# Down projection of a SwiGLU block staged through five buffers instead of two, on one Trainium2 core

## The chip, the cores and the metric

The kernel runs on one core of one Trainium2 chip. The metric is the time of one execution in device microseconds; the number compared is the median of several runs. A profile of one further execution gives the rows shown below. TensorE (PE in the profile) multiplies, VectorE (DVE), ScalarE (ACT) and GpSimd (POOL) do the rest, and SyncE (SP), ScalarE and GpSimd issue DMAs.

## The reference

One layer of a decoder trunk, everything in float32, 512 tokens of width 2048:

```
h = rmsnorm(x);  x = x + concat(diff_attention(h), gated_retention(h)) @ w_o
x = x + cross_attention(rmsnorm(x), rmsnorm(mem))           # 256 memory tokens, 4 heads
hf = rmsnorm(x)
x = x + (silu(hf @ w_gate) * (hf @ w_up)) @ w_down          # D_FF = 5632
out = rmsnorm(x) * norm_f_g
```

The change concerns the last two lines and the hand-over to them.

## The kernel before

**Precision.** Each float32 operand is split into a high part, rounded to fp32r, and the rest: `split(hi, lo, src)` is a cast on ScalarE (L181) and a subtraction on VectorE (L182). A product is three matmuls (`mm3`, L190 to L192).

**Order.** The program order of each engine is what the code emits; no scheduler reorders it. The code builds a list of steps, `plan`, each of which uses one chunk of weights (512 KB). `run_plan` goes through it: first it emits loads (SP, L251) and the splits of weights up to two steps ahead (`split_more`), then the matmuls of the step (`use`), then for the last chunk of a group the evacuation of its PSUM banks (`evac`), and then it advances the generators in `side` by one yield each (`step_side`). A load goes into one of three raw buffers of 4 KB per partition, which comes free once the chunk in it has been split. Split weights of the feed-forward part have three places, so a split waits for the matmuls of the chunk three places before it.

**Feed-forward part.** D_FF is cut into eleven blocks of 512 columns (NB = 11). The order of blocks is gate 0, up 0, then for each b: gate b, down b-1, up b, and at the end gate 10, up 10, down 9, and down 10 fused with the final norm (`finish`).

- Gate and up are done with seven products per pair of k tiles (`seven_products`, matmuls of 256 columns at L888, eight chunks of 42 matmuls each). Their weights are combined and split in `combine_weights` (L266 to L272). The seven sums lie in seven PSUM banks until `fin` adds them on ScalarE and VectorE (L909 and L941, L899, L902). `plan_up` puts them in scratch: two stretches of `rest` at 12 and 14 KB (tag `u`) and the tile `live["u"]`. A generator (`rest_of`) then multiplies by the activated gate, splits the product into `a_h` and `a_l`, and sets `live["a_done"]`.
- Down of block b has four groups of 512 output columns, two chunks each, and four token tiles t with a bank each. The matmuls are 512 columns wide (`a_h`, `a_l` in the profile's names), 48 to a group. In the second chunk the token tiles come one after the other, so that their sums end one after the other. `fin` evacuates one: a scaled copy on ScalarE into a staging buffer (L974), and then an accumulating DMA from it, 256 KB into `y_d` in HBM, issued on GpSimd (L975).
- The staging buffer is `tmp()`: two buffers of 2 KB per partition at 28 and 30 KB of `rest`, taken in turn.
- All of gate, up and down take PSUM banks from one ring of eight (`any_bank`). Up after down takes first the four banks of down's third group and then three of its fourth.

**The end.** The last five steps (chunks of down 9) have eight chunks of down 10 interleaved in the list of loads and splits (`plan_last`). `finish` then loads `y_d` back, 1 MB per token tile (L999), multiplies down 10 (192 matmuls), adds (L1018), squares, normalises and stores (L1030). Its tiles for `y_d` take the memory that `live["u"]`, `a_h`, `a_l` and the third place had.

**The hand-over.** `turn_x` is a generator that transposes x to token order into `y_d`: four groups c of four transposes for each token tile t (L867), a copy (L870) and a DMA on GpSimd (L871). The fourth group has one bank (`spare`, bank 7), as gate 0 holds the others, and runs beside the first chunks of gate 0.

Of the kernel before, what the change touches and what calls it, by code (L numbers as in the profile page):

```python
# [20 lines left out]
P = 128  # L21
D = 2048
KT = D // P
T = 512
# [5 lines left out]
NB = DFF // 512  # L30
# [9 lines left out]
KB = 1024  # L40
# [38 lines left out]
def hybrid_block_kernel(ctx, tc, specs, x_t, mem_t, gains, norm_f_g, weights, alibi, decay, out):  # L79
# [9 lines left out]
    rest = const.tile([P, F_SIZE // 4], F32, name="rest")  # L89
# [1 line left out]
    xpool = top.enter_context(tc.tile_pool(name="xpool", bufs=1))  # L91

    bank = [psum.tile([P, 512], F32, name=f"bank{i}") for i in range(8)]
    turn = {"acc": 0, "aux": 0, "any": 0, "tmp": 0, "st": 0, "xst": 0, "yss": 0}

    def take(tag, n):
        turn[tag] += 1
        return (turn[tag] - 1) % n
# [10 lines left out]
    def shaped(flat, shape):  # L109
        if len(shape) == 2:  # L110
            return flat
        names = "abcd"[:len(shape) - 1]
        return flat.rearrange("p (" + " ".join(names) + ") -> p " + " ".join(names),
                              **dict(zip(names[1:], shape[2:])))

    def part(arena, at, shape):
        n = int(np.prod(shape[1:]))
        return shaped(arena[:, at // 4:at // 4 + n], shape)
# [56 lines left out]
    def tmp():  # L175
        return part(rest, F_TMP + take("tmp", 2) * 2 * KB, [P, T])
# [124 lines left out]
    def step_side():  # L301
        for g in list(side):
            if next(g, "end") == "end":
                side.remove(g)
# [47 lines left out]
    def cols(name, *pieces, row0=0):  # L352
        return lambda k0, nk: chunk(name, row0 + k0 * P, nk, pieces)
# [25 lines left out]
    def token_major(w, width, nk_total, lhs_of, ntok, finish, hook=None, bank=acc, ffn=False):  # L379

        nk = 1024 // width
        banks = {}
        for k0 in range(0, nk_total, nk):
            last = k0 + nk >= nk_total

            def use(hi, lo, k0=k0, last=last):
                for a, b in order(nk, ntok, last):
                    kk, t = (b, a) if last else (a, b)
                    if k0 == 0 and kk == 0:
                        banks[t] = bank(name="tm")  # L390
                    c = kk * width
                    mm3(banks[t][:, :width], lhs_of(k0 + kk, t), (hi[:, c:c + width], lo[:, c:c + width]),
                        k0 + kk == 0, k0 + kk == nk_total - 1)
            add(w(k0, nk), use,
                (lambda: [finish(t, banks[t]) for t in range(ntok)]) if last else None, hook if last else None, ffn=ffn)
# [129 lines left out]
    live = {}  # L525
# [330 lines left out]
    def spare(name=""):  # L856
        return bank[7]

    def turn_x():

        for c in range(4):
            while prep["ready"] < 4 * c + 4:
                yield
            for t in range(NT):
                ps = (acc if c % 2 == 0 else aux)() if c < 3 else spare()
                for k in range(4):
                    nc.tensor.transpose(ps[:, k * P:(k + 1) * P], xT[4 * c + k][:, t * P:(t + 1) * P], ident)  # L867
                yield
                st = tmp()
                nc.scalar.copy(st, ps)  # L870
                nc.gpsimd.dma_start(out=y_d[t * P:(t + 1) * P, c * 512:(c + 1) * 512], in_=st)  # L871
        live["turned"] = True
# [91 lines left out]
    def plan_down(b):  # L964
        for c0 in range(0, D, 512):
            def lhs(k, t):
                while live["a_done"] < b:
                    step_side()
                a = live["late"]
                return a[0][:, k, t * P:(t + 1) * P], a[1][:, k, t * P:(t + 1) * P]  # L970

            def fin(t, ps, c0=c0):
                st = tmp()
                nc.scalar.activation(st, ps, AF.Copy, scale=rx[:, t:t + 1])  # L974
                nc.gpsimd.dma_start(out=y_d[t * P:(t + 1) * P, c0:c0 + 512], in_=st, accum_op=ALU.add)  # L975
            token_major(cols("w_down", (c0, 512), row0=b * 512), 512, 4, lhs, NT, fin, bank=any_bank, ffn=True)
# [56 lines left out]
    def before(f):  # L1033
        marks.append((len(plan), f))
# [23 lines left out]
    def begin_pairs():  # L1058
        live.update(turned=False, late=None, g_done=-1, a_done=-1)
        start_prepare(prepare_pairs, G_FFN)  # L1060
        side.append(turn_x())
# [6 lines left out]
    def begin_late():  # L1068
        while not live["turned"] or prep["gen"] in side:
            step_side()  # L1070
        top.close()
        late = top.enter_context(tc.tile_pool(name="late", bufs=1))
        live["u"] = late.tile([P, 2, 256], F32, name="u3")
        live["late"] = [late.tile([P, 4, T], F32R, name=n) for n in ("a_h", "a_l")]
        third = late.tile([P, 14 * KB // 4], F32R, name="third")
        places["seven"].insert(0, (0, 14 * KB, third))

    before(begin_ffn)
    plan_gate(0)
    before(lambda: turn.update(any=8))  # L1080
    plan_up(0)
    marks.append((len(plan) - 5, begin_late))
    for b in range(1, NB):
        plan_gate(b)
# [58 lines left out]
```

## Time and profile before

| | |
|---|---|
| median of 3 runs | 2820.25 us (2817.19 to 2822.77) |
| the profiled execution | 2818.68 us, of which the span is 2816.3 us |
| mean granted TensorE clock | 0.985 |
| TensorE busy | 2707.0 us (96%) |
| VectorE busy | 1679.0 us (60%) |
| ScalarE busy | 1122.0 us (40%) |
| GpSimd busy | 150.4 us (5%) |
| evacuations of down (L974) | 160, 689 ns each |
| accumulating DMAs into `y_d` (L975, with 16 plain ones of L871) | 176, 256 KB, 5.4 us from issue to landing (median) |
| weight loads (L251) | 519, 512 KB, 3.4 us |

Busy times overlap, so they don't add up to the span. A matmul's end is modelled, so that a row of matmuls is best read from start to start. The rows that the prediction quotes are from the page, from lists of waits (who waited for whom: total us, times, longest us), from instructions in order of time (start, duration, and in brackets the idle time before and what ended it), and from stretches of time cut out of the trace.

### The profile page before, as it was taken

The numbers are of one execution on the slowest core, as the hardware profiler recorded it, in microseconds if no ns is written. First come the engines' busy times: TensorE is split into PE (matmuls) and PEld (weight loads), VectorE is DVE, ScalarE is ACT, GpSimd is POOL, SyncE is SP. The second block draws the span as 40 slices with busy tenths as digits, with TensorE's granted clock in tenths as the row PEclk, the third lists the DMA queues.
The fourth block names the chain that finished last, engine by engine and source line by source line (L and its number), as shares of the span: only waits on it lengthen the run. The fifth ranks groups of instructions, "written<-read, shape, count | busy, mean of one in ns | idle before, by whom it ended". The sixth has DMA issues, their size and how long they took to land.

```text
span 2816.3 us, 41803 instructions
## 1 busy us (share of the span) xinstructions
PE 2707.0 (96%) x17078; PEld 2449.3 (87%) x17078; DVE 1679.0 (60%) x2494; ACT 1122.0 (40%) x1550; POOL 150.4 (5%) x186
## 2 busy tenths in 40 slices
PE   9999999999999999999998999998989989999997
PEld 8999988888888888887898989898888979798985
DVE  6676444544554445746984756657475848484855
ACT  6555423333332223534534443443443434434433
POOL 0000000000000000000001010110101010101011
PEclk9999999999999999999999999999999999999998
DMA  7877642222222222233236364554546363637255
GB/s 243 291 243 235 219 164 83 89 88 89 95 90 95 88 96 89 90 100 117 98 111 144 110 146 120 128 127 126 132 113 152 109 142 120 143 106 150 98 151 170
DMA packets 124128, 373.16 MB, mean 132 GB/s; under 512 B 13472, under 2 KB 23712, under 8 KB 123424
## 3 DMA queue, kind: packets, MB, share of 16 engines
q1 hardware_dynamic: 96848, 314.88, 33.7%
q0 software_dynamic: 24640, 47.20, 11.4%
q10 hardware_dynamic: 2448, 8.43, 0.7%
q8 instruction: 133, 2.18, 0.3%
q14 instruction: 59, 0.48, 0.1%
HBM read 303.34 MB, written 67.11 MB: 132 GB/s over the span
## 4 chain that ended last, share of the span: by engine, by line
PE 46%; issue 41%; DVE 5%; POOL 5%; ACT 2%; DMA 1%; POOLq 0%; ACTq 0%; DVEq 0%
PE bank L190 15%; PE bank L192 15%; PE bank L191 15%; POOL y_d L975 5%; PE bank L888 1%; ACT ops L270 1%; DMA y_d<-rest 1%; DVE ops L272 1%; DVE rest L266 0%; DVE y L1018 0%; DVE rest L899 0%; DVE ops L182 0%; DMA rest<-in_norm_f_g_dram 0%; DVE rest L268 0%; DVE rest L269 0%
## 5 line engine op out<-in xcount | busy, mean ns | idle before, releaser
L190 PE MATMUL bank<-ops 128*128 128x512 f32 (+1 forms) x2504 | 858.4, 343 | 12.6 <-ACT ops L181 7.2
L191 PE MATMUL bank<-ops 128*128 128x512 f32 (+1 forms) x2504 | 851.3, 340 | 0.8 <-DVE ops L182 0.8
L192 PE MATMUL bank<-ops 128*128 128x512 f32 (+1 forms) x2504 | 851.7, 340 | 0.0
L182 DVE TENSOR_TENSOR ops<-rest,ops 128x1024 fp32r<-128x1024 f32 (+1 forms) x380 | 449.8, 1188 | 630.8 <-ACT ops L181 617.3
L888 PE MATMUL bank<-ops 128*128 128x256 f32 x5208 | 650.6, 285 | 66.1 <-ACT rest L974 56.4
L888 PEld LDWEIGHTS bank<-ops 128*128 128x128 f32 x5208 | 635.6, 193 | 76.6 <-ACT rest L974 60.8
L181 ACT CAST ops<-rest 128x1024 fp32r<-128x1024 f32 (+1 forms) x380 | 386.0, 1022 | 686.1 <-PE bank L191 354.1
L190 PEld LDWEIGHTS bank<-ops 128*128 128x128 f32 x2504 | 473.4, 189 | 69.1 <-ACT ops L181 8.1
L192 PEld LDWEIGHTS bank<-ops 128*128 128x128 f32 x2504 | 472.7, 189 | 53.8 <-DVE ops L182 0.2
L191 PEld LDWEIGHTS bank<-ops 128*128 128x128 f32 x2504 | 473.2, 189 | 52.8 <-DVE ops L182 1.4
L888 PE MATMUL bank<-ops,third 128*128 128x256 f32 x2184 | 265.5, 280 | 2.7 <-ACT rest L941 1.6
L888 PEld LDWEIGHTS bank<-ops,third 128*128 128x128 f32 x2184 | 260.4, 189 | 3.1 <-ACT rest L941 1.8
L974 ACT ACTIVATE rest<-bank,small 128x512 f32<-128x512 f32 x160 | 109.4, 689 | 288.9 <-DMA y_d<-rest 268.4
L270 ACT CAST ops<-rest 128x1024 fp32r<-128x1024 f32 x124 | 130.3, 1051 | 224.2 <-DVE rest L269 182.7
L975 POOL DMA_DIRECT2D y_d<-rest x160 | 138.7, 881 | 1271.3 <-ACT rest L974 1151.0
L271 DVE TENSOR_TENSOR ops<-rest,ops 128x768 fp32r<-128x768 f32 x124 | 118.2, 953 | 102.6 <-ACT ops L267 88.4
L272 DVE TENSOR_TENSOR ops<-rest,ops 128x1024 fp32r<-128x1024 f32 x124 | 152.0, 1226 | 31.0 <-ACT ops L270 29.2
L190 PE MATMUL bank<-ops,a_h 128*128 128x512 f32 x408 | 160.2, 393 | 4.0 <-ACT ops L181 4.0
L191 PE MATMUL bank<-ops,a_h 128*128 128x512 f32 x408 | 160.1, 393 | 0.5 <-DVE ops L182 0.5
L192 PE MATMUL bank<-ops,a_l 128*128 128x512 f32 x408 | 159.7, 391 | 0.0
L267 ACT CAST ops<-rest 128x768 fp32r<-128x768 f32 x124 | 103.4, 834 | 88.5 <-issue 51.8
L266 DVE TENSOR_TENSOR rest<-rest 128x512 f32<-128x512 f32 x176 | 121.4, 690 | 4.2
(138 smaller groups left out, 2062.9 us busy)
## 6 DMA issues: line engine op xcount, KB each, us to landing
rest<-in_weights_dram SPq DMA_DIRECT2D x519, 512.0 KB, 3.4
y_d<-rest POOLq DMA_DIRECT2D x176, 256.0 KB, 5.4
h_d<-rest ACTq DMA_DIRECT2D x16, 512.0 KB, 5.5
g_d<-rest SPq DMA_DIRECT2D x32, 256.0 KB, 5.1
rest<-g_d SPq DMA_DIRECT2D x16, 512.0 KB, 3.2
rest<-h_d SPq DMA_DIRECT2D x16, 512.0 KB, 3.3
xT<-in_x_t_dram SPq DMA_DIRECT2D x16, 256.0 KB, 5.8
y<-y_d SPq DMA_DIRECT2D x4, 1024.0 KB, 7.5
```

The lines of the kernel that those rows point to most:

```text
L181: nc.scalar.copy(hi, src)
L182: nc.vector.tensor_tensor(out=lo, in0=src, in1=hi.bitcast(F32), op=ALU.subtract)
L190: nc.tensor.matmul(out_ap, lh, rh, start=first, stop=False)
L191: nc.tensor.matmul(out_ap, lh, rl, start=False, stop=False)
L192: nc.tensor.matmul(out_ap, ll, rh, start=False, stop=last)
L266: nc.vector.tensor_tensor(out=w[:, 0:2], in0=q[:, 1:3], in1=q[:, 0:1].to_broadcast([P, 2, 256]), op=ALU.add)
L270: nc.scalar.copy(hi[:, 3:7], w)
L271: nc.vector.tensor_tensor(out=lo[:, 0:3], in0=q[:, 1:4], in1=hi[:, 0:3].bitcast(F32), op=ALU.subtract)
L272: nc.vector.tensor_tensor(out=lo[:, 3:7], in0=w, in1=hi[:, 3:7].bitcast(F32), op=ALU.subtract)
L888: nc.tensor.matmul(to, x[:, b, c], y[:, a], start=j == 0 and o == 0 and m == 0, stop=j == nj - 1 and m == 2, skip_group_check=True)
L974: nc.scalar.activation(st, ps, AF.Copy, scale=rx[:, t:t + 1])
L975: nc.gpsimd.dma_start(out=y_d[t * P:(t + 1) * P, c0:c0 + 512], in_=st, accum_op=ALU.add)
```

## The change

Down's evacuation takes its staging buffer from a ring of five: the two of `tmp()`, the two stretches of `rest` that up uses for its sums, and `live["u"]`. Before it does so it makes sure that up's generator has read its sums; only for the last down (block 9, which follows up 10) is there something left to emit. The transposes of the fourth group of `turn_x` begin one step later.

```
-    turn = {"acc": 0, "aux": 0, "any": 0, "tmp": 0, "st": 0, "xst": 0, "yss": 0}
+    turn = {"acc": 0, "aux": 0, "any": 0, "stage": 0, "tmp": 0, "st": 0, "xst": 0, "yss": 0}
...
 def turn_x():
         for c in range(4):
             while prep["ready"] < 4 * c + 4:
                 yield
+            if c == 3:
+                yield
             for t in range(NT):
...
 def plan_down(b):
             def fin(t, ps, c0=c0):
-                st = tmp()
+                while live["a_done"] < (b if b < NB - 2 else NB - 1):
+                    step_side()
+                st = live["stages"][take("stage", 5)]
                 nc.scalar.activation(st, ps, AF.Copy, scale=rx[:, t:t + 1])
                 nc.gpsimd.dma_start(out=y_d[t * P:(t + 1) * P, c0:c0 + 512], in_=st, accum_op=ALU.add)
...
 def begin_late():
         places["seven"].insert(0, (0, 14 * KB, third))
+        live["stages"] = [part(rest, at * KB, [P, T]) for at in (28, 30, 12, 14)]
+        live["stages"].append(live["u"].rearrange("p a b -> p (a b)"))
```

In the changed file the evacuation stands at L978, its DMA at L979, the load of `y_d` at L1003, the transposes at L869, and the matmuls of gate and up at L890.

ScalarE, first and second group of the first down, with what each instruction waits for. `DMASW0` to `DMASW7` are the semaphores that GpSimd's DMAs signal in turn, `DMAHW` those of the loads; `u_10492` is `live["u"]`. Before:

```order
L974 ACTIVATE rest<-bank_76,small 128x512 [waits PE_49]
L974 ACTIVATE rest<-bank_77,small 128x512 [waits PE_49]
L974 ACTIVATE rest<-bank_70,small 128x512 [waits DMASW0_49,PE_49,Activation_49]
L974 ACTIVATE rest<-bank_71,small 128x512 [waits DMASW1_49,PE_49,Activation_49]
L924 ACTIVATE rest<-rest 128x1024 [waits DVE_49]
L181 CAST third<-rest 128x1024 [waits DMAHW6_49]
L181 CAST ops<-rest 128x1024 [waits DMAHW7_49,PE_49]
L974 ACTIVATE rest<-bank_72,small 128x512 [waits DMASW2_49,PE_49,Activation_49]
L974 ACTIVATE rest<-bank_73,small 128x512 [waits DMASW3_49,PE_49,Activation_49]
```

After:

```order
L978 ACTIVATE rest<-bank_76,small 128x512 [waits PE_49]
L978 ACTIVATE rest<-bank_77,small 128x512 [waits PE_49]
L978 ACTIVATE rest<-bank_70,small 128x512 [waits PE_49]
L978 ACTIVATE rest<-bank_71,small 128x512 [waits PE_49]
L926 ACTIVATE rest<-rest 128x1024 [waits DVE_49]
L181 CAST third<-rest 128x1024 [waits DMAHW6_49,Activation_49]
L181 CAST ops<-rest 128x1024 [waits DMAHW7_49,PE_49,Activation_49]
L978 ACTIVATE u_10492<-bank_72,small 128x512 [waits PE_49]
L978 ACTIVATE rest<-bank_73,small 128x512 [waits DMASW0_49,PE_49,Activation_49]
```

The order is the same; before, the third evacuation waited for the DMA of the first; now the sixth does.

ScalarE at the first group of the last down (block 9), where the two casts `128x2x256` at a time are the halves of up 10's split. Before:

```order
L181 CAST ops<-rest 128x2x256 [waits DVE_49] x2
L181 CAST ops<-rest 128x1024 [waits DMAHW5_49,PE_49,Activation_49]
L974 ACTIVATE rest<-bank_73,small 128x512 [waits DMASW6_49,PE_49]
L974 ACTIVATE rest<-bank_74,small 128x512 [waits DMASW7_49,PE_49]
L974 ACTIVATE rest<-bank_75,small 128x512 [waits DMASW0_49,PE_49,Activation_49]
L974 ACTIVATE rest<-bank_76,small 128x512 [waits DMASW1_49,PE_49,Activation_49]
L181 CAST ops<-rest 128x2x256 [waits DVE_49] x2
```

After:

```order
L181 CAST ops<-rest 128x2x256 [waits DVE_49] x2
L181 CAST ops<-rest 128x1024 [waits DMAHW5_49,PE_49,Activation_49]
L181 CAST ops<-rest 128x2x256 [waits DVE_49] x2
L978 ACTIVATE u_10492<-bank_73,small 128x512 [waits DMASW3_49,PE_49]
L978 ACTIVATE rest<-bank_74,small 128x512 [waits DMASW4_49,PE_49]
L978 ACTIVATE rest<-bank_75,small 128x512 [waits DMASW5_49,PE_49]
L978 ACTIVATE rest<-bank_76,small 128x512 [waits PE_49]
```

The second pair of casts moved ahead of the four evacuations.

SP's queue at the end: the last load of weights, the four loads of `y_d` and the first store. Before:

```order
L251 DMA rest<-in_weights_dram 128x1024 [waits DMAHW6_49,DVE_49]
L999 DMA y_21595<-y_d 128x2048 [waits DMASW4_49,DMASW0_49,PE_49]
L999 DMA y_21596<-y_d 128x2048 [waits DMASW5_49,DMASW1_49]
L999 DMA y_21597<-y_d 128x2048 [waits DMASW6_49,DMASW2_49]
L999 DMA y_21598<-y_d 128x2048 [waits DMASW7_49,DMASW3_49]
L1030 DMA out_dram<-rest 128x512 [waits DVE_49]
```

After:

```order
L251 DMA rest<-in_weights_dram 128x1024 [waits DMAHW6_49,DVE_49]
L1003 DMA y_21595<-y_d 128x2048 [waits DMASW4_49,DMASW3_49,DMASW5_49,DMASW2_49,DMASW6_49,DMASW1_49,DMASW7_49,DMASW0_49,Activation_49]
L1003 DMA y_21596<-y_d 128x2048 [waits DMASW5_49,DMASW1_49]
L1003 DMA y_21597<-y_d 128x2048 [waits DMASW6_49]
L1003 DMA y_21598<-y_d 128x2048 [waits DMASW3_49]
L1034 DMA out_dram<-rest 128x512 [waits DVE_49]
```

The first load takes memory that is now the fifth stage, and waits for the last accumulating DMAs of all token tiles; the three others stand behind it.

More of the change, by code (lines that the diff above doesn't have):

```diff
@@ L93, in hybrid_block_kernel @@
     bank = [psum.tile([P, 512], F32, name=f"bank{i}") for i in range(8)]
-    turn = {"acc": 0, "aux": 0, "any": 0, "tmp": 0, "st": 0, "xst": 0, "yss": 0}
+    turn = {"acc": 0, "aux": 0, "any": 0, "stage": 0, "tmp": 0, "st": 0, "xst": 0, "yss": 0}
     def take(tag, n):
@@ L863, in turn_x @@
                 yield
+            if c == 3:
+                yield
             for t in range(NT):
@@ L972, in fin @@
             def fin(t, ps, c0=c0):
-                st = tmp()
+                while live["a_done"] < (b if b < NB - 2 else NB - 1):
+                    step_side()
+                st = live["stages"][take("stage", 5)]
                 nc.scalar.activation(st, ps, AF.Copy, scale=rx[:, t:t + 1])
@@ L1076, in begin_late @@
         places["seven"].insert(0, (0, 14 * KB, third))
+        live["stages"] = [part(rest, at * KB, [P, T]) for at in (28, 30, 12, 14)]
+        live["stages"].append(live["u"].rearrange("p a b -> p (a b)"))
     before(begin_ffn)
```

## The prediction

> **What bounds the kernel now.** I read the page first (shares, groups), then the waits, then the order of time on TensorE and ScalarE around one down projection, then stretches and DMA queues there.
>
> ```profile
> span 2816.3 us, 41803 instructions
> ...
> PE 2707.0 (96%) x17078; PEld 2449.3 (87%) x17078; DVE 1679.0 (60%) x2494; ACT 1122.0 (40%) x1550; POOL 150.4 (5%) x186
> ...
> L974 ACT ACTIVATE rest<-bank,small 128x512 f32<-128x512 f32 x160 | 109.4, 689 | 288.9 <-DMA y_d<-rest 268.4
> ```
>
> TensorE is the bound, but "busy" hides slow matmuls. The odd row is L974: 160 evacuations of down, before which ScalarE sits idle for 268.4 us because a staging buffer is still being read by its DMA. ScalarE is 40% busy, so that alone costs nothing; the question is who stands behind it. From TensorE's waits between 1400 and 2760 us (total, times, longest):
>
> ```profile
> PE bank L888 <- ACT rest L974: 56.4, 21, 5.4
> ```
>
> The products of gate and up (L888) wait 56.4 us for banks that down's evacuations hold. One such place, on TensorE:
>
> ```profile
> 1600.79 0.40 PE L190 MATMUL bank<-ops,a_h 128*128 128x512 f32 x1
> ...
> 1644.37 3.12 PE L888 MATMUL bank<-ops 128*128 128x256 f32 x24
> 1649.17 1.68 PE L888 MATMUL bank<-ops 128*128 128x256 f32 x12 [1.69 <-ACT rest L974]
> 1655.59 7.45 PE L888 MATMUL bank<-ops 128*128 128x256 f32 x48 [4.74 <-ACT rest L974]
> 1662.88 5.11 PE L888 MATMUL bank<-ops,third 128*128 128x256 f32 x42
> ```
>
> Down's 192 matmuls run from 1600.79 to 1644.37: 43.6 us, 0.227 each, 10.9 per group of four evacuations, with no hole. Then up starts, and after four of its seven banks it stops. The same place on ScalarE:
>
> ```profile
> 1607.85 0.69 ACT L974 ACTIVATE rest<-bank,small 128x512 f32<-128x512 f32 x1 [0.27 <-PE bank L192]
> ...
> 1654.85 0.69 ACT L974 ACTIVATE rest<-bank,small 128x512 f32<-128x512 f32 x1 [5.14 <-DMA y_d<-rest]
> 1656.11 0.69 ACT L974 ACTIVATE rest<-bank,small 128x512 f32<-128x512 f32 x1 [0.58 <-DMA y_d<-rest]
> ```
>
> These are the first and the last two of sixteen evacuations: 1607.85 to 1656.80, 12.2 us a group behind a TensorE that needs 10.9. The last ends 12.4 us after up's first matmul. Two buffers don't keep the pace, and up pays.
>
> **Part 1, the starts of up 1 to 9.** Nine stretches of 20 us, each from the end of a down (the first, the emptiest and the last are shown; columns: time, TensorE busy and its matmuls, granted clock, DMA share, GB/s), and a tenth where nothing waits:
>
> ```profile
> 1511.20:1531.20 20.00, 12.48 (x77) 0.83 0.83 146
> ...
> 2040.60:2060.60 20.00, 11.87 (x76) 0.83 0.85 149
> ...
> 2569.40:2589.40 20.00, 14.32 (x103) 0.91 0.87 155
> 1670.00:1690.00 20.00, 20.00 (x172) 1.00 0.31 108
> ```
>
> The nine hold 788 matmuls (76 to 103 each); the undisturbed one holds 172, or 170 without the two that its edges cut. 9 x 170 - 788 = 742 missing, at 20/170 = 0.118 us each: 87 us. That exceeds the 56.4 us of waits because the clock after a hole is granted only in part: the 48 matmuls from 1655.59 take until 1662.88, 7.3 us instead of 5.7. [...]
>
> With five buffers an evacuation needs the DMA of the fifth before it, about a whole group (10.9 us) back. What a DMA takes, in the stretch 1596 to 1666 us (queue's packets, MB, share of 16 engines; then issues, KB, median us to landing), and what POOL takes to issue one (ns, min/median/max):
>
> ```profile
> q0 software_dynamic: 2304, 4.20, 43.6%
> q1 hardware_dynamic: 1744, 6.32, 27.6%
> ...
> rest<-in_weights_dram SPq DMA_DIRECT2D x12, 512.0 KB, 4.8
> y_d<-rest POOLq DMA_DIRECT2D x16, 256.0 KB, 5.5
> L975 POOL DMA_DIRECT2D y_d<-rest x160: 856/865/1178, 1475.6 to 2767.8; - x160
> ```
>
> Landing takes 5.5 us, four issues 3.5 us of 10.9: no wait for a buffer is left. Evacuations then follow the sums, which the last chunk of a group completes 6 x 0.227 = 1.36 us apart. Token tile 0 of the last group leaves its bank some 3.4 us before down ends, and up's fifth product wants it 24 x 0.118 = 2.8 us after: 6 us of room, 5 for tile 2. Late next would be the weight split for up's third chunk, behind the last evacuation on ScalarE: it starts 1 us after down ends, takes about 3, and is wanted at 9.9. Bounds: 87, or 60 if splits keep a third of the holes; I take 86, since every step has microseconds of room.
>
> Up's first sum now waits for stages too, but the down before it ended eight chunks (40 us) earlier against a landing of 5.5: nothing.
>
> **Part 2, the last down (block 9).** Its first evacuations now stand behind the whole split of up 10, two more casts and the products that feed them: some 3 us. The same banks are wanted two groups on, which hides it; without that cover it costs those 3. It gains elsewhere:
>
> ```profile
> 2720.00:2730.00 10.00, 10.00 (x46) 8.18 (x44) 1.58 (x2) 2.22 (x3) 1.76 (x2) 1.00 0.86 226
> 2730.00:2740.00 10.00, 5.50 (x14) 3.76 (x12) 3.72 (x5) 4.60 (x8) 1.73 (x2) 0.72 0.76 164
> ...
> 2734.30 0.79 PE L190 MATMUL bank<-ops,a_h 128*128 128x512 f32 x1 [4.03 <-ACT ops L181]
> ```
>
> (Columns from TensorE busy on: weight loads, VectorE, ScalarE, POOL, clock, DMA share, GB/s.) TensorE waits for a weight cast queued behind a blocked evacuation: 14 matmuls where 46 fit, 7 us. Thirteen weight loads share this down with its 16 accumulates, so part may return as late weights: 2 to 7, I take 6.
>
> **Part 3, the end.**
>
> ```profile
> 2748.94 0.39 PE L190 MATMUL bank<-ops 128*128 128x512 f32 x1
> 2766.80 0.69 ACT L974 ACTIVATE rest<-bank,small 128x512 f32<-128x512 f32 x1 [1.62 <-DMA y_d<-rest]
> DMA to landing us min/median/max: 7.0/7.5/9.5
> 2802.37 0.75 DVE L1018 SCALAR_TENSOR_TENSOR y<-bank,small,y 128x512 f32<-128x512 f32 x1
> 2806.54 0.74 DVE L1018 SCALAR_TENSOR_TENSOR y<-bank,small,y 128x512 f32<-128x512 f32 x1
> ```
>
> The third row is y's four loads. Call Z the end of the last down (2748.9). Now its last evacuation ends at Z+18.6 and the span at Z+67.4. After the change: evacuation Z+1.0, accumulate 5.6 more, then the loads of y, all of them, as the first now waits for the last accumulate too: 7.0, so VectorE begins at Z+13.6. A token tile takes it two times 4.17 us (four L1018 with their neighbours, then the norm), about 8.5: tile 3 starts at Z+39. Its last sum needs TensorE's 192 matmuls, Z+43.6. From the last L1018 to the end stand 9.8 us: Z+53.6, a gain of 13.8. With a slow load (9.5) and a slow accumulate VectorE is some 5 later: 9. I take 12, near the clean end, since the two engines nearly tie.
>
> **Part 4, the transposes.** The last four go one chunk later each, their copies and DMAs with them (POOL is idle there).
>
> ```profile
> 1338.72 0.66 PE L867 MATMUL bank<-ident,xT 128*128 128x128 f32 x4 [1.88 <-ACT rest L870]
> 1331.00:1358.00 27.00, 22.58 (x189) 21.83 (x188) 24.64 (x36) 17.20 (x24) 1.63 (x3) 1.00 0.32 107
> ```
>
> The wait of 1.88 us for the first copy goes, but VectorE, busy for 24.6 of these 27 us, sets the pace of splits and copies, and the next copy is late instead: between -2 and +1.5, I take 0.
>
> **Sum.** 86 + 6 + 12 + 0 = 104 us, off the profiled execution's 2818.7 (span 2816.3 and 2.4 around it): 2714.7. The median of the runs shown is 1.6 above that execution: 2716.
>
> **Rivals.** *The DMA engines become the bound.* From the queue rows, 43.6% of 70 us over 16 accumulates is 1.91 us of all engines each, 27.6% over 12 loads 1.61: a down needs 16 x 1.91 + 8 x 1.61 = 43.4 of its 43.6 us once nothing slows the stream. [...] For it: those shares. Against it: 6.32 + 4.20 MB in 70 us are 150 GB/s, and the page's second slice moves 291, so part of the packet time must be waiting.
>
> ```profile
> GB/s 243 291 243 235 219 164 83 89 88 89 95 90 95 88 96 89 90 100 117 98 111 144 110 146 120 128 127 126 132 113 152 109 142 120 143 106 150 98 151 170
> ```
>
>  It decides above 2.2 us an accumulate; at 2.4 a stage ends 7.7 us late, 5 of room taken off leaves 2.7 idle and as much for the clock, 5 x 9 = 48 us lost: 2764. *Slower than before:* weight loads starve TensorE inside down. Three raw buffers and 5.45 us a chunk give a load some 12 us against 4.8 now; to eat 104 us over 72 chunks, 1.45 each, loads must land in 12 + 3 x 1.45 = 16.4; from there it decides, and at 17 it gives 2836. The row is against it: that is over three times the present landing. *The staging isn't the cause:* evacuations wait for casts instead of DMAs and the holes stay. Then only parts 2 and 3 come: 2802; if these too go to late weights, 2820. The waits' row names the DMA, which leaves little for it.
>
> **How the numbers follow.** The forecast (parts 1 to 4 within their bounds, up to a third of part 1 lost) 0.81; everything at its best or better, under 2706, 0.03; DMA engines in part the bound 0.10; holes stay, faster through the end alone, 0.01, or no change 0.02; starved 0.03. All terms at their best give 87 + 7 + 14 + 2 = 110, 2710; low is 4 below, as the edges of nine stretches hide some four matmuls each: 2706. All at their worst give 60 + 2 + 9 - 1.5 = 69.5, 2751; since that is unlikely together, high is 2744, and with the DMA case and the rest under 2 in 10 are left out. A measurement of this kernel tells 0.2% (5.6 us) from nothing; faster 0.95, within 0.02, slower 0.03.
>
> **What would show it.** Right: the evacuations (L978 then) wait on DMAs for under 20 us; about 170 matmuls in 20 us at clock 1.00 after each down; no hole in the last down; the span ends 54 to 58 us after it. Wrong: a DMA share near 1 in down with landings over 10 us, evacuations waiting for sums or casts at the same banks, or a new wait of TensorE for casts inside down.

## The result, and the profile after

The changed kernel takes 2719.26 us (median of 4 runs, 2718.65 to 2719.92) against 2820.82 us before (4 runs): a ratio of 0.9641, 95% interval 0.9625 to 0.9658, 3.6% faster. The forecast was 2716. Span of the profiled execution: 2717.7 us against 2816.3, 98.6 less, where 104 was forecast. All times compared here are of undisturbed executions; only of the run with the second store, below, two of six executions were left out (4259 and 5900 us), and no trace of these two was kept.

The page after: span, busy time by engine, the shares of the chain that ended last, and the row of the evacuations (128 of the 160; the other 32 go into `live["u"]`).

```profile
span 2717.7 us, 41832 instructions
...
PE 2677.0 (99%) x17078; PEld 2428.4 (89%) x17078; DVE 1683.8 (62%) x2494; ACT 1121.3 (41%) x1550; POOL 150.2 (6%) x186
...
PE 85%; issue 7%; DVE 5%; ACT 2%; DMA 1%; POOL 0%; ACTq 0%; DVEq 0%; POOLq 0%
...
L978 ACT ACTIVATE rest<-bank,small 128x512 f32<-128x512 f32 x128 | 87.4, 688 | 63.1 <-PE bank L192 60.6
```

TensorE is busy for 99% and makes up 85% of the chain. What ends the idle time before an evacuation is now TensorE's sum (L192) and no longer a DMA. On ScalarE, the last group of the same down as in the prediction's lines, which show its last two evacuations before the change (1654.85 and 1656.11):

```profile
1630.59 0.68 ACT L978 ACTIVATE rest<-bank,small 128x512 f32<-128x512 f32 x1
1631.63 0.69 ACT L978 ACTIVATE u<-bank,small 128x512 f32<-128x512 f32 x1 [0.35 <-ACT rest L978]
1632.99 0.69 ACT L978 ACTIVATE rest<-bank,small 128x512 f32<-128x512 f32 x1 [0.67 <-PE bank L192]
1634.35 0.69 ACT L978 ACTIVATE rest<-bank,small 128x512 f32<-128x512 f32 x1 [0.67 <-PE bank L192]
```

The last three are 1.36 us apart, as the sums are; up starts at 1634.10, so the last ends 0.9 us after it instead of 12.4. And the stretches of 20 us after the first and the last of the nine downs, with an undisturbed one below (TensorE busy and matmuls, granted clock, DMA share, GB/s):

```profile
1511.90:1531.90 20.00, 20.00 (x173) 1.00 0.64 154
...
2488.90:2508.90 20.00, 20.00 (x173) 1.00 0.66 155
1660.00:1680.00 20.00, 20.00 (x174) 1.00 0.26 85
```

No hole is left and no clock is lost: 173 matmuls where 77 and 103 stood, and the seven stretches between read the same, 173 at 1.00. The end is another matter. TensorE's first matmul of the last down and VectorE's first use of `y_d`, before the change; then TensorE's first matmul of the last down and the first one after it, after the change:

```profile
2697.45 0.39 PE L190 MATMUL bank<-ops,a_h 128*128 128x512 f32 x1
...
2771.54 0.75 DVE L1018 SCALAR_TENSOR_TENSOR y<-bank,small,y 128x512 f32<-128x512 f32 x1 [11.95 <-DMA y<-y_d]
```

```profile
2608.80 0.39 PE L190 MATMUL bank<-ops,a_h 128*128 128x512 f32 x1
2653.63 0.39 PE L190 MATMUL bank<-ops 128*128 128x512 f32 x1
```

The last down begins 88.7 us earlier, takes 44.8 us instead of 51.5 (before, it ended at 2748.94), and from its end to the end of the span stand 64.1 us instead of 67.4. Of the changed kernel's end, in the order ScalarE, ScalarE, SP, VectorE:

```profile
2659.69 1.14 ACT L181 CAST ops<-rest 128x512 fp32r<-128x512 f32 x2 [5.71 <-DMA rest<-in_weights_dram]
2660.73 1.84 ACT L978 ACTIVATE rest<-bank,small 128x512 f32<-128x512 f32 x3
2671.94 2.16 SPq L1003 DMA_DIRECT2D y<-y_d  x4
2678.03 0.75 DVE L1022 SCALAR_TENSOR_TENSOR y<-bank,small,y 128x512 f32<-128x512 f32 x1 [16.39 <-DMA y<-y_d]
```

The last four evacuations stand behind a cast of down 10's weights that waits 5.71 us for its load. They start 7.1 us after the down's end, y's loads are issued at 18.3, and VectorE starts at 24.4: later than before (22.6), not sooner. The end is 3.3 us shorter all the same, because VectorE takes 39.7 us from its start to the end of the span instead of 44.8.

### The profile page after: what moved, and what is told of

It reads as the page before. It is cut to its first block, busy times and chain, and to the rows that moved or that the text cites. A ratio compares the mean times of both kernels' runs of the same rounds, so it can differ in the third digit from the quotient of the medians.

```text
span 2717.7 us, 41832 instructions
## 1 busy us (share of the span) xinstructions
PE 2677.0 (99%) x17078; PEld 2428.4 (89%) x17078; DVE 1683.8 (62%) x2494; ACT 1121.3 (41%) x1550; POOL 150.2 (6%) x186
## 4 chain that ended last, share of the span: by engine, by line
PE 85%; issue 7%; DVE 5%; ACT 2%; DMA 1%; POOL 0%; ACTq 0%; DVEq 0%; POOLq 0%
PE bank L890 24%; PE bank L190 20%; PE bank L192 20%; PE bank L191 20%; ACT ops L270 1%; DVE ops L272 1%; POOL y_d L979 0%; DVE rest L266 0%; DVE y L1022 0%; DVE rest L901 0%; DVE ops L182 0%; DVE rest L268 0%; DVE rest L269 0%; DMA rest<-in_norm_f_g_dram 0%; DVE ssq L498 0%
## 5 line engine op out<-in xcount | busy, mean ns | idle before, releaser
L190 PE MATMUL bank<-ops 128*128 128x512 f32 (+1 forms) x2504 | 859.2, 343 | 12.2 <-ACT ops L181 6.1
L192 PE MATMUL bank<-ops 128*128 128x512 f32 (+1 forms) x2504 | 852.5, 340 | 0.0
L890 PE MATMUL bank<-ops 128*128 128x256 f32 x5208 | 624.5, 280 | 4.9 <-DVE ops L271 2.9
L890 PEld LDWEIGHTS bank<-ops 128*128 128x128 f32 x5208 | 616.3, 188 | 8.1 <-DVE ops L271 3.8
L192 PEld LDWEIGHTS bank<-ops 128*128 128x128 f32 x2504 | 473.5, 189 | 54.0 <-DVE ops L182 0.2
L890 PE MATMUL bank<-ops,third 128*128 128x256 f32 x2184 | 264.1, 279 | 3.1 <-ACT rest L943 1.6
L890 PEld LDWEIGHTS bank<-ops,third 128*128 128x128 f32 x2184 | 258.7, 188 | 3.7 <-ACT rest L943 1.8
L979 POOL DMA_DIRECT2D y_d<-rest x128 | 112.7, 907 | 899.6 <-ACT rest L978 895.1
L192 PE MATMUL bank<-ops,a_l 128*128 128x512 f32 x408 | 158.7, 389 | 0.0
L978 ACT ACTIVATE rest<-bank,small 128x512 f32<-128x512 f32 x128 | 87.4, 688 | 63.1 <-PE bank L192 60.6
```

Of the source, the lines that this page charges most:

```text
L190: nc.tensor.matmul(out_ap, lh, rh, start=first, stop=False)
L192: nc.tensor.matmul(out_ap, ll, rh, start=False, stop=last)
L890: nc.tensor.matmul(to, x[:, b, c], y[:, a], start=j == 0 and o == 0 and m == 0, stop=j == nj - 1 and m == 2, skip_group_check=True)
```

## The experiments

**The two parts apart.** Five stages without the later transposes (the two lines with `c == 3` left out):

> Five stages, the transposes as before. Theory: the later transposes cost the changed kernel 0.7 us (gate and up of block 0 start at 1398.71 instead of 1398.03) and the ring has no part in that, so this one is within 1 us of the changed kernel's 2719.3, at about 2718.6. Rival: the later transposes matter for what follows; then it is over 2722 or under 2715.

Measured: 2719.99 us, ratio 0.9648 (0.9635 to 0.9660), against 0.9641 for the changed kernel. Then the kernel before with those two lines alone:

> Two stages as before, only the fourth group of transposes one chunk later. Theory: 2820.8 plus 0 to 1, within 0.2% of the kernel before. Rival, that the hand-over gives part of the gain: under 2815.

Measured: 2818.85 us, ratio 0.9998 (0.9989 to 1.0006). The whole gain is the ring's; the later transposes make no measurable difference. The 0.7 us that the profiled execution showed at their place does not come back in the times; in other profiles with the later transposes the first down starts between 1467.0 and 1468.0 (four stages, six raw buffers), against 1467.5 before.

**How many stages.** Four, without `live["u"]` (u3 in the expectation):

```
-                st = live["stages"][take("stage", 5)]
+                st = live["stages"][take("stage", 4)]
...
-        live["stages"].append(live["u"].rearrange("p a b -> p (a b)"))
```

> The changed kernel with four stages, without the tile u3. On the nine starts of up, theory: a buffer is free again 0.7 + 0.2 + 6 = 7 us after its evacuation starts, so n buffers carry n evacuations in 7 us; four carry a group in 7 of the 10.9 us that TensorE needs, so these starts stay without holes (about 170 matmuls in 20 us). On the end two theories differ: if the loads of y are late because the first must wait for the last accumulate (its memory is the fifth stage), then without that stage VectorE starts some 4 us earlier after the last down and the time is about 2715; if they are late because the last evacuations stand behind weight casts that wait for their loads, the time stays at 2719 within 2 us.

Measured: 2719.28 us, ratio 0.9644 (0.9632 to 0.9656): as good as five. For the end it decided between the two theories. SP's first load of y and VectorE's first use of it:

```profile
2667.99 5.71 SPq L1003 DMA_DIRECT2D y<-y_d  x4
2678.48 0.75 DVE L1022 SCALAR_TENSOR_TENSOR y<-bank,small,y 128x512 f32<-128x512 f32 x1 [15.89 <-DMA y<-y_d]
```

Its last down ends at 2654.74, so the first load is issued at 13.3 us after it instead of 18.3, yet VectorE starts at 23.7 instead of 24.4. The added wait of the first load on all accumulates is real and costs next to nothing: issued sooner, the load takes 10.4 us to land instead of 6.0. The four loads of the final gain, which GpSimd issues at 10.8 to 12.6 us in both kernels, then land at 19.5 to 25.7 us instead of 18.9 to 20.8; no run tests whether these and the loads of y hold each other up.

Three stages (28, 30 and 12 KB):

> The changed kernel with three stages. Theory of the pace: three buffers carry a group in 4/3 x 7 = 9.3 us, less than the 10.9 that TensorE needs, so the gain at the starts of up stays whole and the time is 2719 to 2725. Rival, that it takes five, as a group's four evacuations must each find a buffer of their own: holes stay at the starts of up, and the time is between 2740 and 2800.

Measured: 2751.04 us, ratio 0.9756 (0.9743 to 0.9768). The time is the rival's, but the place is not. Wait list, ScalarE in two groups of a down and at the start of the following up, and TensorE:

```profile
ACT rest L978 <- DMA y_d<-rest: 184.0, 48, 6.1
```

```profile
1735.92 0.69 ACT L978 ACTIVATE rest<-bank,small 128x512 f32<-128x512 f32 x1 [0.67 <-PE bank L192]
1741.07 0.69 ACT L978 ACTIVATE rest<-bank,small 128x512 f32<-128x512 f32 x1 [4.46 <-DMA y_d<-rest]
...
1765.89 0.69 ACT L978 ACTIVATE rest<-bank,small 128x512 f32<-128x512 f32 x1 [4.56 <-DMA y_d<-rest]
...
1771.24 1.06 ACT L270 CAST ops<-rest 128x1024 fp32r<-128x1024 f32 x1 [2.26 <-DVE rest L269]
1775.29 1.05 ACT L270 CAST ops<-rest 128x1024 fp32r<-128x1024 f32 x1 [2.26 <-DVE rest L269]
```

```profile
1758.79 9.96 PE L890 MATMUL bank<-ops 128*128 128x256 f32 x84
...
1820.03 9.98 PE L890 MATMUL bank<-ops 128*128 128x256 f32 x82 [1.40 <-DVE ops L271]
```

Up starts at 1758.79 without a hole, as the pace said. But a group's four evacuations come within 4.1 us (3 x 1.36) and a buffer is busy for some 7 (6.4 to 9.2 where a fourth evacuation of this down waits for it), so the fourth waits about 4 us for the first's DMA: 48 waits, 3.8 us on average. The casts of up's weights then stand behind the last one, which starts 7.1 us after up (1765.89); in the changed kernel it starts 0.25 us after up. They follow at 4.05 us a chunk where TensorE takes 4.90, so the lag shrinks by 0.85 a chunk and outlives up; TensorE pays in the gate behind it. Against the profile of the changed kernel, the nine blocks from the end of the first down to the start of the last lose 2.1 us each on average, 18.7 in all, the last down 6.5 (51.3 us, almost as with two) and the end 4.1; 1.2 went the other way ahead of them. That is the 28.1 us between the two spans; the profiled execution is the fastest of the four. Four is what it takes: then a buffer was last used for the same token tile one group earlier, 10.9 us back.

**The end.** Two remedies for the casts ahead of the last evacuations. One emits the last two splits behind them:

```
-            split_more(plan[min(i + SPLITS_AHEAD, len(plan)) - 1]["item"] + 1 + 2 * max(0, i + SPLITS_AHEAD - len(plan)))
+            ahead = plan[min(i + SPLITS_AHEAD, len(plan)) - 1]["item"] + 1 + 2 * max(0, i + SPLITS_AHEAD - len(plan))
+            split_more(ahead if i < len(plan) - 1 else ahead - 2)
...
+        split_more(len(items))
```

> The changed kernel, but in its last step of the plan the splits of the last two chunks of weights stand behind the four evacuations instead of ahead of them. In the changed kernel the last evacuations start 7.1 us after the last down ends, behind a cast that waits 5.7 us for its load; y's loads are issued at 18 us, VectorE starts at 24 us and the span ends at 64 us after it. Theory, that this order is what keeps the end long: the last evacuation starts about 0.7 us after the down, VectorE at 16, TensorE ends the final matmuls unhindered, the span ends at 56 and the time is about 2711. Rival, that the DMA engines are what is late there (their share is 0.92 to 1.03): evacuations come earlier but their accumulates and y's loads land later, and the time stays at 2717 to 2720.

Measured: 2715.49 us, ratio 0.9628 (0.9615 to 0.9642): 3.8 us better than the changed kernel, less than half of the 8.3 that the theory said. The last three evacuations on ScalarE:

```profile
2654.57 0.69 ACT L980 ACTIVATE rest<-bank,small 128x512 f32<-128x512 f32 x1 [2.65 <-DMA y_d<-rest]
2656.25 0.69 ACT L980 ACTIVATE rest<-bank,small 128x512 f32<-128x512 f32 x1 [1.00 <-DMA y_d<-rest]
2658.42 0.69 ACT L980 ACTIVATE u<-bank,small 128x512 f32<-128x512 f32 x1 [1.48 <-DMA y_d<-u]
```

With the casts out of the way they wait for stages: the group before had come in a cluster, behind another late cast. The last evacuation starts 4.8 us after the last down ends (forecast 0.7), VectorE at 17.5 (16), and the span ends at 59.4 (56). The other remedy takes the cause of the late casts away, the lack of raw buffers:

```
             def fin(t, ps, c0=c0):
                 while live["a_done"] < (b if b < NB - 2 else NB - 1):
                     step_side()
+                if b == NB - 2 and c0 == 0 and t == 0:
+                    raw_free.extend(part(rest, at * KB, [P, 1024]) for at in (0, 4, 8))
```

> The changed kernel with three more raw buffers for weight loads from the first evacuation of the last down on, in scratch that gate and up no longer need; the order of casts and evacuations is that of the changed kernel. Theory, that the last evacuations are late only because the casts ahead of them wait for loads that found no raw buffer: casts don't wait, the last evacuation starts within 2 us of the last down's end, the hole of 1.2 us in that down goes, and the time is about 2710. Rival, that the engines move no more in that stretch: loads are issued earlier but land as late, and the time stays at 2717 to 2720.

Measured: 2709.34 us, ratio 0.9606 (0.9593 to 0.9619). ScalarE's waits for loads of weights, over the whole kernel, first in the changed kernel (where one more, of 6.7 us, is for a cast into the third place) and then in this one:

```profile
ACT ops L181 <- DMA rest<-in_weights_dram: 18.0, 7, 5.7
```

```profile
ACT ops L181 <- DMA rest<-in_weights_dram: 3.2, 3, 2.4
```

The end of this one, on ScalarE, SP and VectorE:

```profile
2652.32 0.69 ACT L980 ACTIVATE u<-bank,small 128x512 f32<-128x512 f32 x1 [0.67 <-PE bank L192]
2660.32 1.97 SPq L1005 DMA_DIRECT2D y<-y_d  x4
2667.53 0.75 DVE L1024 SCALAR_TENSOR_TENSOR y<-bank,small,y 128x512 f32<-128x512 f32 x1 [17.24 <-DMA y<-y_d]
```

The last down ends at 2652.07 after 43.5 us, without a hole; the last evacuation ends 0.94 us later, y's loads are issued at 8.3, VectorE starts at 15.5, and the span (2707.3) ends 55.2 after it, close to the prediction's 1.0, 6.6, 13.6 and 53.6. It was the loads' issue and not the DMA engines: the last load of weights is issued 15.3 us before the last down ends instead of 2.5, and between 2608 and 2654 us the loads land in 7.6 us (median) in both kernels. Both remedies together:

> The changed kernel with both: the last two splits behind the last evacuations, and three more raw buffers. Theory: the remedies are for the same wait, so together they give no more than 2 us over the better one: about 2709. Rival: they add up, and the time is under 2706.

Measured: 2708.54 us, ratio 0.9604 (0.9591 to 0.9618); the span ends 54.1 us after the last down. One wait, two remedies; they don't add up. This version is faster than both kernels.

**Do the DMA engines come near to being the bound?**

```
+    z_d = dram.tile([T, D], F32, name="z_d")
...
                 nc.gpsimd.dma_start(out=y_d[t * P:(t + 1) * P, c0:c0 + 512], in_=st, accum_op=ALU.add)
+                nc.gpsimd.dma_start(out=z_d[t * P:(t + 1) * P, c0:c0 + 512], in_=st)
```

> The changed kernel, and each evacuated buffer is also stored plainly to a second place in HBM (160 more stores of 256 KB, issued on GpSimd), so that a down moves 16 x 256 KB more. Theory, that the DMA engines have room (150 GB/s of 291 seen elsewhere): no hole at the starts of up, the time within 10 us of 2719, the addition coming from the last down and the end. Rival, that packet time is a true bound: a down would need 16 x (1.69 + 1.4) + 8 x 1.56 = 62 us of all engines in 43.6, 18 us late per block, and the time would be over 2850.

Measured: ratio 0.9652 (0.9636 to 0.9668), four executions of 2721.6 to 2723.4 us. From 1590 to 1660 us, GpSimd's queue (packets, MB, share of 16 engines) and the issues (median us to landing), first of the changed kernel and then of this one, with a start of up ahead of them:

```profile
q0 software_dynamic: 2304, 4.20, 38.6%
...
rest<-in_weights_dram SPq DMA_DIRECT2D x14, 512.0 KB, 4.1
y_d<-rest POOLq DMA_DIRECT2D x13, 256.0 KB, 6.1
```

```profile
1635.00:1655.00 20.00, 20.00 (x174) 1.00 0.71 211
...
q0 software_dynamic: 3584, 8.39, 51.6%
...
rest<-in_weights_dram SPq DMA_DIRECT2D x14, 512.0 KB, 6.3
y_d<-rest POOLq DMA_DIRECT2D x13, 256.0 KB, 8.8
z_d<-rest POOLq DMA_DIRECT2D x13, 256.0 KB, 9.6
```

With twice the stores everything lands later, by 2 to 3 us, and TensorE notices nothing at the starts of up: a down still takes 43.5 us. Nor does a store have a fixed price in packet time: 38.6% of 70 us over 16 accumulates is 1.69 us each, 51.6% over 32 stores 1.13; no run shows the 1.4 us that the expectation puts on a plain store by itself. In the kernel before, the 16 plain ones of L871, with no accumulate beside them from 1240 to 1470 us, took 4.9% of 230 us, 0.70 each. The extra 2 to 4 us of time agree with the end (66.3 us instead of 64.1 after the last down).

## Why the prediction was right, point by point

- **The sum.** 104 us were forecast for the span and 98.6 measured. That it came so near is in part luck: parts 1 and 2 gave 4.1 us more than their terms, parts 3 and 4 gave 9.4 less. Of the four signs of being right two came: no evacuation waits for a DMA any more, and after each of nine downs 173 matmuls stand in 20 us at clock 1.00. Two did not: TensorE has a hole of 0.8 us in the last down, behind a late cast, and the span ends 64.1 us after that down, not 54 to 58.
- **Part 1, 86 us (60 to 87): mechanism right, 89.4 measured.** The last down begins 88.7 us earlier, and 0.7 was lost ahead of the blocks. Mechanism and place came as told, the clock too: in the nine stretches before, what was not granted (0.09 to 0.26 of 20 us) adds up to 29 us, which with 56.4 of waits makes 86. The measured gain lies 2 us over the upper end because the prediction counted an undisturbed stretch as 170 matmuls; with the 173 that now stand there the same sum gives 89 (9 x 173 - 788 = 769, at 20/173 us).
- **Part 2, 6 us (2 to 7): right, 6.7 measured.** The second pair of casts ahead of the first evacuations cost TensorE nothing: with six raw buffers and the same order the down takes 43.5 us, without a hole.
- **Part 3, 12 us (9 to 13.8): wrong, 3.3 measured.** The step that failed is "After the change: evacuation Z+1.0". The last evacuation ended at Z+9.5 (2663.15). The prediction took the ring for the only thing between the last sums and their evacuation. Casts of weights stand there too, in ScalarE's order, and wait for loads that three raw buffers don't let out in time. Part 2 names late weights as a risk for that down; part 3 then took an end near the clean one, and its lower bound allowed only for a slower landing. With the loads let out (six raw buffers) the end is 55.2 us long against the 53.6 worked out, a gain of 12.2, so the rest of that chain was sized well; from VectorE's start to the end it said 40.0, and 39.7 came. The new wait of the first load of y, which part 3 put into the chain, is no measurable cost of its own (2719.28 us without it, with four stages).
- **Part 4, 0 (-2 to +1.5): right**, 0.7 lost in one profile, nothing in the times.
- **The rivals.** DMA engines as the bound: no, shown by the second store; the shares of packet time of before (43.4 of 43.6 us) were no limit, as twice the stores fitted into the same 43.5 us, and dividing them up made the case look nearer than it was. That an idle us costs as much again in clock, in this rival's 48 us, was the author's estimate and no run shows it: before, 29 us of clock not granted stood beside 56.4 of waits. Weights that starve TensorE inside down: only in the last one, and slightly (44.8 us against 43.5). Holes that stay because evacuations wait for casts: not at the starts of up, but this is what held the last evacuations.
- **The room of "a whole group back".** Right for four and five. The expectation written for three stages used the mean pace (9.3 against 10.9 us a group) and was wrong by 26 us or more, because evacuations come in bursts.

What stays open: why the first load of y, let go 5 us earlier with four stages, landed hardly earlier. That the accumulates and the loads of the final gain were in its way is argued from their times, not tested.

## What to carry to other kernels

Size a staging ring by its burst: count the evacuations that come within one buffer's busy time (here four within 4.1 us against some 7 us), and not by the mean pace, which three buffers met while the kernel still lost 1.2%. When an engine works in program order, a removed wait is gone only if nothing else in its queue waits ahead of the same work: here the last evacuations merely changed from a DMA's wait to a load's, and the end gave 3 us of the 14 worked out, and 12 once the loads got buffers. Price a hole in TensorE by the matmuls missing in a stretch and not by the idle time (56 us of waits were worth 89): here the clock was granted only in part after it, 0.74 to 0.91 over the stretches of 20 us.

## What the runs showed of the hardware that was not expected

The share of DMA packet time did not tell how much more the DMA engines could move. Ten us within the last down of the changed kernel, the whole of that down (2608 to 2654 us), and the same whole with six raw buffers (busy time of TensorE, weight loads, VectorE, ScalarE and GpSimd, granted clock, DMA share, GB/s):

```profile
2639.00:2649.00 10.00, 9.23 (x40) 7.19 (x39) 2.52 (x3) 4.22 (x7) 1.15 (x2) 1.00 0.92 245
2608.00:2654.00 46.00, 45.23 (x203) 37.10 (x202) 23.30 (x32) 22.96 (x36) 10.61 (x12) 1.00 0.71 170
```

```profile
2608.00:2654.00 46.00, 46.00 (x207) 38.18 (x207) 24.65 (x35) 27.01 (x42) 13.75 (x17) 1.00 0.82 202
```

The DMA engines moved 19% more there (202 against 170 GB/s), mostly accumulates that came sooner (16 instead of 12 are issued in this stretch), and the loads' median time to landing stayed at 7.6 us, though the changed kernel's share already reads 0.92 within this stretch. In the second store's run 160 additional stores of 256 KB cost 2.3 to 4.1 us in all (2721.6 to 2723.4 against 2719.26), 0.08 to 0.15%.
